# Values of the first two mLSTM heads in a buffer of their own, projected between the last HGRN steps

## The chip, the cores and the metric

One core of a Trainium2 chip runs the kernel. The metric is the device time of one execution in microseconds (us). Engines are named as in the profile: PE (matrix), DVE (vector), ACT (scalar), POOL (GpSimd), and SP, whose queue issues nearly all the DMAs.

## The reference

One layer of a diffusion backbone over 256 context and 1024 latent tokens of width 1024. Inputs are normalised and modulated by vectors that come from the conditioning, go through two bidirectional recurrent mixers of four heads each (HGRN2 and mLSTM), are mixed by an output matrix, and then go through PEER, a retrieval of single-neuron experts.

```python
def _modulate(x, shift, scale):
    return _layer_norm(x) * (1 + scale) + shift
...
o_hg_c, o_hg_l = _bidirectional(_gla_chunkwise, ...)
qk_l = jax.nn.silu(_conv_grid(jnp.concatenate([mq_l, mk_l], axis=-1), conv_w, conv_b))
h_ml_c, h_ml_l = _bidirectional(
    _mlstm_chunkwise, ml_shared(qk_c, mv_c), ml_shared(qk_l, mv_l),
    _mlstm_gates(mgt_c, gate_b), _mlstm_gates(mgt_l, gate_b))
...
x <- LN(alpha*x + gate1 * W_out [HGRN2 heads | mLSTM heads](modulate(LN(x))))
x <- LN(alpha*x + gate2 * PEER(modulate(LN(x))))
```

The mLSTM gates take a log-sigmoid of half of 16 gate columns; query and key of the mLSTM go through a 3x3 convolution over a 64-wide grid ahead of the recurrence; the values (mv) do not.

## The kernel before

The stages follow each other in program text, but the framework decides each engine's order with a timeline of its own, so work of one stage may lie in another's as far as buffers allow.

- `modcols` loads the first 2048 columns of w_mod (8 tiles of 1 MB) and multiplies them with the two conditioning vectors: 3 of 4 column blocks on PE, the fourth on DVE. Its result is `modc`, without which no token tile can be modulated. Two of the ten token tiles `xt` are loaded ahead of the weights, eight behind.
- `inputs_ln` normalises the tiles, transposes them on PE, modulates them on ACT into `xf`, and DVE and POOL write the pair `xmT` (fp16 high part, bf16 rest). Every projection runs three passes over high and low parts (`proj_f` with 512-column matmuls, line 222; `proj_t` with 256, line 230).
- A class `W` loads one 1 MB block of weights into `wf` and splits it: ACT casts the high part (line 76), POOL subtracts the rest (line 77). The blocks are named after their columns: HI, HQ, HF0, HF1, HG for HGRN, MQ, MK, MV, MO for the mLSTM.
- `gates` makes the mLSTM's gate rows on [64, 1280] tiles: transposes, log-sigmoid by three activations, scans on DVE; then 30 small transposes and 8 small matmuls (lines 331, 337) bring them back into columns.
- `modrows` multiplies the other 4096 columns of w_mod, 32 tiles of 512 KB in a buffer `wm` of its own, with 128 matmuls (line 686).
- `hgrn` projects values and runs 8 head-directions, each: gate projection, ACT functions (first `sg`, line 394), scan, and a recurrence on PE and DVE.
- `mlstm` projects values into one tile `mv` (`values(0)` for heads 0 and 1, `values(1)` for 2 and 3: 240 matmuls and 10 copies on ACT each). `qkproj` then copies query and key into `pad` (line 545) and convolves them with nine passes on DVE (lines 553 and 555). `one` runs the recurrence; POOL scales keys into `kw` (line 589) and adds the backward part to `acm` (line 647) from a single buffer `tm`. `ro.hg` and `ro.ml` are the readout's gates.
- `mix_weights` loads w_out by fourths into `wof` (three buffers), scales and splits it; `mix_out` and `peer` follow.
- `uprep` prepares 128 slices of PEER's table in spare time: load 512 KB into `us` (two buffers), ACT cast (line 198), POOL subtract (line 199), store `Ud`. 96 of them are called by `hgrn` and `mlstm` in program text; where they run is the framework's choice, in the same order on ACT, POOL and SP.

Of the kernel before, what the change touches and what calls it, by code (L numbers as in the profile page):

```python
# [236 lines left out]
def gates(g, I, w):  # L237
    nc, tc = g.nc, g.tc
    gp = g.gp
    with tc.tile_pool(name="gt", bufs=1, reuse_waits="tile") as tp:  # L240
        gb = tp.tile([128, 16], F32, name="gb")
        nc.sync.dma_start(gb, rowb(I["ml_gate_b"], 0, 16))
        ps = g.pp.tile([128, 512], F32, name="oa")
        for t in range(NT):
            proj_t(g, w, t, ps[:, t * 16:(t + 1) * 16])
        gt = tp.tile([128, NT, 2, 64], F32, name="gt")
        nc.vector.memset(gt, 0.0)
        psv = ps[:, :NT * 16].rearrange("p (t a d h) -> p t a d h", a=2, d=2, h=4)
        gbv = gb.rearrange("p (a d h) -> p a d h", a=2, d=2)
        for a in range(2):  # L250
            for d in range(2):
                nc.vector.tensor_tensor(gt[:, :, a, 32 * d:32 * d + 4], psv[:, :, a, d, :],
                                        gbv[:, None, a, d, :].to_broadcast([128, NT, 4]), op=OP.add)
        rows = []
        for a in range(2):
            r = tp.tile([64, SQ], F32, name=f"row{a}")
            for t0 in range(0, NT, 4):
                n = min(4, NT - t0)
                pt = g.pp.tile([128, 512], F32, name="sc")
                for i in range(n):  # L260
                    nc.tensor.transpose(pt[0:64, i * 128:(i + 1) * 128], gt[:, t0 + i, a, :], g.ident)
                nc.vector.tensor_copy(r[:, t0 * 128:(t0 + n) * 128], pt[0:64, :n * 128])
            rows.append(r)
        ir, fr = rows
        e = tp.tile([64, SQ], F32, name="ge")
        nc.scalar.activation(e, fr, AF.Abs)
        nc.scalar.activation(e, e, AF.Exp, scale=-1.0)
        nc.scalar.activation(e, e, AF.Ln, bias=1.0)
        lf = fr
        nc.vector.scalar_tensor_tensor(lf, fr, 0.0, e, op0=OP.min, op1=OP.subtract)  # L270
        one = tp.tile([64, NT, 128], F32, name="one")
        neg = tp.tile([64, NT, 128], F32, name="neg")
        nc.vector.memset(one, 1.0)
        nc.vector.memset(neg, 0.0)
        nc.vector.memset(one[:, :, 0:1], 0.0)
        nc.vector.memset(neg[:, :, 0:1], -BIG)
        oneF, negF = (x.rearrange("p t s -> p (t s)") for x in (one, neg))
        a = tp.tile([64, NT, 128], F32, name="ga")
        aF = a.rearrange("p t s -> p (t s)")
        nc.vector.tensor_tensor_scan(aF[0:32], oneF[0:32], lf[0:32], 0.0, op0=OP.mult, op1=OP.add)  # L280
        nc.vector.tensor_tensor_scan(aF[32:64, ::-1], oneF[32:64], lf[32:64, ::-1], 0.0, op0=OP.mult, op1=OP.add)
        gqF = ir
        gq = ir.rearrange("p (t s) -> p t s", s=128)
        nc.vector.tensor_sub(gqF, ir, aF)
        M = tp.tile([64, NT, 128], F32, name="gM")
        MF = M.rearrange("p t s -> p (t s)")
        nc.vector.tensor_tensor_scan(MF[0:32], negF[0:32], gqF[0:32], 0.0, op0=OP.add, op1=OP.max)
        nc.vector.tensor_tensor_scan(MF[32:64, ::-1], negF[32:64], gqF[32:64, ::-1], 0.0, op0=OP.add, op1=OP.max)
        G = tp.tile([64, NT], F32, name="gG")
        al = tp.tile([64, NT], F32, name="gal")  # L290
        nc.vector.tensor_copy(G[0:32], M[0:32, :, 127])
        nc.vector.tensor_copy(G[32:64], M[32:64, :, 0])
        nc.vector.tensor_copy(al[0:32], a[0:32, :, 127])
        nc.vector.tensor_copy(al[32:64], a[32:64, :, 0])
        mn = tp.tile([64, NT], F32, name="gmn")
        mp_ = tp.tile([64, NT], F32, name="gmp")
        nc.vector.tensor_tensor_scan(mn[0:32], G[0:32], al[0:32], 0.0, op0=OP.max, op1=OP.add)
        nc.vector.tensor_tensor_scan(mn[32:64, 1::-1], G[32:64, 1::-1], al[32:64, 1::-1], 0.0, op0=OP.max, op1=OP.add)
        nc.vector.tensor_tensor_scan(mn[32:64, :1:-1], G[32:64, :1:-1], al[32:64, :1:-1], mn[32:64, 0:1],
                                     op0=OP.max, op1=OP.add)  # L300
        nc.vector.memset(mp_, 0.0)
        nc.vector.tensor_copy(mp_[0:32, 1:NT], mn[0:32, 0:NT - 1])
        nc.vector.tensor_copy(mp_[32:64, 0:1], mn[32:64, 1:2])
        nc.vector.tensor_copy(mp_[32:64, NT - 1:NT], mn[32:64, 0:1])
        nc.vector.tensor_copy(mp_[32:64, 2:NT - 1], mn[32:64, 3:NT])
        ml = tp.tile([64, NT], F32, name="gml")
        nc.vector.tensor_max(ml, G, mp_)
        mpb = mp_[:, :, None].to_broadcast([64, NT, 128])
        nc.vector.tensor_tensor(M, M, mpb, op=OP.max)
        negM = tp.tile([64, LAT], F32, name="negM")  # L310
        nc.vector.tensor_scalar(negM, MF[:, CTX:], -1.0, None, op0=OP.mult)
        nc.sync.dma_start(g.negM, negM)
        win = tp.tile([64, LAT], F32, name="win")
        wv = fr.rearrange("p (t s) -> p t s", s=128)
        nc.vector.tensor_tensor(wv, mpb, M, op=OP.subtract)
        nc.scalar.activation(win, wv.rearrange("p t s -> p (t s)")[:, CTX:], AF.Exp)
        nc.sync.dma_start(g.win, win)
        ws = e.rearrange("p (t s) -> p t s", s=128)
        nc.vector.tensor_tensor(ws, gq, ml[:, :, None].to_broadcast([64, NT, 128]), op=OP.subtract)
        nc.scalar.activation(ws, ws, AF.Exp)  # L320
        cd = tp.tile([64, NT], F32, name="gcd")
        nc.vector.tensor_sub(cd, mp_, ml)
        nc.scalar.activation(cd, cd, AF.Exp)
        fl = a
        nc.vector.tensor_add(fl, a, M)
        nc.scalar.activation(fl, fl, AF.Exp, scale=-1.0)
# [1060 lines left out]
```

## Time and profile before

| what | us |
|---|---|
| median of 3 runs | 3220.53 (3216.59 to 3222.46) |
| profiled execution, its time | 3223.63 |
| profiled execution, its span | 3221.9 |
| mean granted clock of PE | 0.953 of full speed |
| PE busy in the span | 2938.5 |
| DVE busy in the span | 2611.8 |

The span runs from the first to the last instruction. About the first 886 us belong to the stages that the change touches; the part behind them is PEER and its preparation. Busy times are those of one execution.

### The profile page before, as it was taken

Reading aid. Unit: us, or ns where it says so; the run is one execution under the profiler, and the core shown is the slowest. Engines: PE = TensorE matmul, PEld = TensorE weight load, DVE = VectorE, ACT = ScalarE, POOL = GpSimd, SP = SyncE. Lnnn points to the kernel's source line nnn. Section 1 sums busy time; section 2 is a strip of 40 time slices with the busy share of each in tenths; the row PEclk is TensorE's granted clock in tenths of the full one; section 3 lists DMA queues with packets and bytes.
Section 4 is the critical chain, followed back from the end, with each engine's and each line's share of the span. In section 5 each row is a group of like instructions: output and inputs, shape, how many; then the busy total and the mean of one; then the engine's idle time right before and its main releaser. Section 6 shows DMA issues by size and latency. Waiting matters only on the chain.

```text
span 3221.9 us, 50811 instructions
## 1 busy us (share of the span) xinstructions
PE 2938.5 (91%) x18943; PEld 1892.4 (59%) x18943; DVE 2611.8 (81%) x5352; ACT 1181.8 (37%) x1699; POOL 1846.0 (57%) x1358
## 2 busy tenths in 40 slices
PE   7898989888898799799999989999999999999985
PEld 4644556657786567577777875555555555554432
DVE  8434464999878899888877777898999998988998
ACT  4465563324345532126666653222222222222111
POOL 3555675422347465416566665676666666666664
PEclk8899998898899899899999999999999999999987
DMA  7688666421267689758889998999999999999994
GB/s 282 213 289 291 213 207 232 139 64 55 103 221 268 210 324 331 288 176 279 300 278 297 307 345 324 355 368 364 359 364 360 360 354 366 355 347 336 342 327 183
DMA packets 319548, 900.33 MB, mean 279 GB/s; under 512 B 28076, under 2 KB 107572, under 8 KB 311364
## 3 DMA queue, kind: packets, MB, share of 16 engines
q1 hardware_dynamic: 208708, 494.38, 43.3%
q0 software_dynamic: 110592, 402.70, 34.2%
q8 instruction: 149, 2.44, 0.3%
q14 instruction: 99, 0.81, 0.1%
HBM read 758.67 MB, written 138.30 MB: 278 GB/s over the span
## 4 chain that ended last, share of the span: by engine, by line
PE 42%; DVE 24%; DMA 11%; POOL 9%; issue 9%; ACT 4%; SPq 0%; DVEq 0%; POOLq 0%; ACTq 0%
PE y L1164 16%; PE S L1131 12%; DMA row<-in_peer_v_dram,idx 5%; POOL row L1072 4%; DVE row L1091 3%; PE pj L222 3%; DVE mz L555 3%; PE pj L230 2%; DVE us L1034 2%; POOL vs L1147 2%; DMA us<-in_peer_ut_dram 2%; DMA row<-in_peer_u_dram,idx 2%; DVE hg L1099 2%; POOL uT L199 2%; PE y L1039 1%
## 5 line engine op out<-in xcount | busy, mean ns | idle before, releaser
L1164 PE MATMUL y<-vs,w 128*128 128x512 bf16 x3840 | 878.9, 382 | 40.5 <-POOL vs L1147 16.6
L1131 PE MATMUL S<-hTd,uT 128*128 128x320 f16 (+1 forms) x6144 | 898.6, 300 | 10.7 <-issue 6.2
L1131 PEld LDWEIGHTS <-uT 128*128 128x128 bf16 x6144 | 602.6, 98 | 276.0 <-issue 13.2
L1164 PEld LDWEIGHTS <-w 128*128 128x128 bf16 x3840 | 378.2, 98 | 471.4 <-issue 61.4
L1099 DVE SCALAR_TENSOR_TENSOR hg<-row,dot,hg 128x1024 f32<-128x1024 f32 x381 | 489.5, 1285 | 110.3 <-DMA row<-in_peer_v_dram,idx 94.7
L1072 POOL DMA_INDIRECT row<-in_peer_u_dram,idx x384 | 387.4, 1009 | 287.2 <-DVE row L1091 135.2
L1072 POOL DMA_INDIRECT row<-in_peer_v_dram,idx x384 | 387.4, 1009 | 219.7 <-DVE hg L1099 133.2
L1091 DVE SCALAR_TENSOR_TENSOR row<-row,hg 128x1024 f32<-128x1024 f32 x384 | 458.7, 1211 | 58.1 <-DMA row<-in_peer_u_dram,idx 52.1
L199 POOL TENSOR_TENSOR uT<-us,uT 128x1024 bf16<-128x1024 f32 x128 | 303.9, 2379 | 188.7 <-ACT uT L198 173.1
L1146 ACT CAST vs<-row 128x1024 bf16<-128x1024 f32 x128 | 133.5, 1043 | 488.7 <-DMA row<-in_peer_v_dram 467.0
L1147 POOL TENSOR_TENSOR vs<-row,vs 128x1024 bf16<-128x1024 f32 x128 | 277.9, 2171 | 28.7 <-ACT vs L1146 23.1
L1035 POOL TENSOR_TENSOR kT<-us,gf 128x512 f32<-128x512 bf16 x160 | 178.3, 1137 | 200.3 <-DVE us L1034 175.5
L222 PE MATMUL pj<-xmT,wb 128*128 128x512 f16 (+3 forms) x1248 | 262.5, 367 | 19.9 <-ACT pad L545 18.5
L1136 ACT ACTIVATE ge<-S 128x320 f32<-128x320 f32 x256 | 111.8, 441 | 408.2 <-PE S L1131 299.5
L230 PE MATMUL pj<-wb,xmT 128*128 128x256 f16 (+1 forms) x1728 | 224.3, 290 | 22.4 <-DVE rsg L748 12.0
L1171 DVE TENSOR_TENSOR ya<-ya,y 128x512 f32<-128x512 f32 x310 | 207.3, 681 | 26.1 <-PE y L1164 24.3
L230 PEld LDWEIGHTS <-xmT 128*128 128x128 f16 (+1 forms) x1968 | 186.6, 103 | 65.0 <-issue 24.1
L222 PEld LDWEIGHTS <-wb 128*128 128x128 f16 (+1 forms) x1248 | 123.8, 101 | 147.7 <-issue 43.3
L1040 ACT COPY gst<-y 128x512 f32<-128x512 f32 x160 | 171.3, 1075 | 83.9 <-PE y L1039 66.0
L1034 DVE TENSOR_TENSOR us<-iob,eT 128x512 bf16<-128x512 bf16 x320 | 172.4, 588 | 14.6 <-ACT kT L1036 9.0
L1039 PE MATMUL y<-kT 128*128 128x128 f32 x1280 | 165.2, 281 | 17.1 <-ACT kT L1036 8.1
L198 ACT CAST uT<-us 128x1024 bf16<-128x1024 f32 x128 | 133.2, 1044 | 122.9 <-DMA us<-in_peer_ut_dram 96.5
(390 smaller groups left out, 3927.8 us busy)
## 6 DMA issues: line engine op xcount, KB each, us to landing
us<-in_peer_ut_dram SPq DMA_DIRECT2D x128, 512.0 KB
Ud<-uT SPq DMA_DIRECT2D x128, 512.0 KB
uT<-Ud SPq DMA_DIRECT2D x128, 512.0 KB
row<-in_peer_v_dram SPq DMA_DIRECT2D x128, 512.0 KB
Gd<-gst SPq DMA_DIRECT2D x20, 1984.0 KB
Gt<-Gd SPq DMA_DIRECT2D x31, 1280.0 KB
Sd<-ge SPq DMA_DIRECT2D x66, 320.0 KB
kT<-Sd SPq DMA_DIRECT2D x66, 320.0 KB
```

The costliest lines, as they stand in the source:

```text
L199: nc.gpsimd.tensor_tensor(lo, uf, hi, op=OP.subtract)
L222: g.nc.tensor.matmul(ps[:, :t1 - t0], w.t[a][:, k, c0:c0 + 128], g.xmT[b][:, k, t0:t1], start=(k == 0 and a == b), stop=(k == KD - 1 and a ...
L230: g.nc.tensor.matmul(ps, g.xmT[a][:, k, t * 128:(t + 1) * 128], w.t[b][:, k, :w.n], start=(k == 0 and a == b), stop=(k == KD - 1 and a == 1))
L1034: nc.vector.tensor_tensor(cm[:, a], g.iob, eT[:, a, None, t0:t0 + 4].to_broadcast([128, 128, 4]), op=OP.is_equal)
L1039: nc.tensor.matmul(ps[:, i * 128:(i + 1) * 128], oh[:, 0, i], oh[:, 1, i], start=True, stop=True)
L1072: d = g.nc.gpsimd.indirect_dma_start(out=b, out_offset=None, in_=self.I["peer_u" if n < 128 else "peer_v"][0], in_offset=bass.IndirectOffs ...
L1091: nc.vector.scalar_tensor_tensor(b, b, 1.0, self.ps, op0=OP.mult, op1=OP.mult, accum_out=dot[:, j:j + 1])
L1099: nc.vector.scalar_tensor_tensor(self.ps, b, dot[:, j:j + 1], self.ps, op0=OP.mult, op1=OP.add)
L1131: m = nc.tensor.matmul(ps[:, :hn], uT[:, a, k, :], g.hTd[b][:, k, i * hn:(i + 1) * hn], start=(k == 0 and (a, b) == (0, 0)), stop=(k == KD ...
L1147: nc.gpsimd.tensor_tensor(v[:, 1], vf, v[:, 0], op=OP.subtract)
L1164: nc.tensor.matmul(ps, w[:, a, t * 128:(t + 1) * 128], v[:, b, h * 512:(h + 1) * 512], start=(n == 0), stop=(n == 3 * GI - 1))
L1171: nc.vector.tensor_add(ya, ya, ps)
```

## The change

- `modcols`: all ten token tiles are loaded ahead of w_mod; all four column blocks go to PE, into one PSUM bank at four partition offsets; four full transposes take the place of the small ones; the weights HI are loaded behind w_mod.
- `inputs_ln`: for odd blocks ACT writes the high part of `xmT` itself, with a second activation, where DVE copied it.
- `gates`: the log-sigmoid runs on [128, 80] before the transposes; transposes alternate between two banks; the small transposes into columns become a function `cols()`, called after both value projections of HGRN.
- `modrows` takes its tiles from the two `us` buffers that `uprep` uses too.
- `values(g, I, 0)` is called at the end of `hgrn` and writes `mv0`, which lies in a pool that outlives both stages; the other half is `mv1`.
- `mix_weights`: the first fourth uses `mv0`'s memory, the others share two buffers.

```diff
+    ps = g.pp.tile([128, 512], F32, name="pj", bufs=2)
+    xs = inputs_load(g, I, lp, 0, NT)
     for k in range(KD):
-        if k == KD // 2:
-            g.w0.append(W(g, I, HI))
         wt = mp.tile([128, 2048], F32, name="w0", bufs=8)
         nc.sync.dma_start(wt, I["w_mod"][0, k * 128:(k + 1) * 128, 0:2048])
-        for b in range(3):
-            nc.tensor.matmul(ps[b][0:2], g.cs[:, k::8], wt[:, b * 512:(b + 1) * 512], start=(k == 0), stop=(k == KD - 1))
...
+        for q in range(4):
+            nc.tensor.matmul(ps[32 * q:32 * q + 2], g.cs[:, k::8], wt[:, q * 512:(q + 1) * 512], start=(k == 0), stop=(k == KD - 1))
+    g.w0.append(W(g, I, HI))
+    for q in range(4):
+        o = slice(32 * q, 32 * q + 2)
+        (nc.scalar.copy if q % 2 else nc.vector.tensor_copy)(mr[o], ps[o])
...
-            nc.vector.tensor_copy(g.xmT[0][:, k, sl], f)
+            if k % 2:
+                nc.scalar.activation(g.xmT[0][:, k, sl], pt[:, :n * 128], AF.Identity, scale=g.modc[:, 8 + k, j:j + 1], bias=g.modc[:, k, j:j + 1])
+            else:
+                nc.vector.tensor_copy(g.xmT[0][:, k, sl], f)
...
+    nc.scalar.activation(e, f, AF.Abs)
+    nc.scalar.activation(e, e, AF.Exp, scale=-1.0)
+    nc.scalar.activation(e, e, AF.Ln, bias=1.0)
...
         inputs(1)
         g.uprep(8)
+        cols()
+        gs.close()
...
+        values(g, I, 0)
+
+
+def values(g, I, b):
+
+    nc = g.nc
+    nc.vector.memset(g.mv[b][:, :, :, 128:129], 1.0)
+    w = W(g, I, MV + 256 * b)
+    for t in range(NT):
+        ps = g.pp.tile([128, 512], F32, name="pj", bufs=2)
+        proj_t(g, w, t, ps[:, :256])
+        nc.scalar.copy(g.mv[b][:, t, :, 0:128], ps[:, :256].rearrange("p (h c) -> p h c", c=128))
...
-                wt = mp.tile([128, 1024], F32, name="wm", bufs=2)
+                wt = g.up.tile([128, 2, D], BF, name="us").rearrange("p a b -> p (a b)").bitcast(F32)
...
+        if h == 0:
+            wf = g.gp.tile([128, NT, 2, 129], F32, name="mv0").rearrange("p a b c -> p (a b c)")[:, 0:KD * 256]
+            wf = wf.rearrange("p (k c) -> p k c", c=256)
+        else:
+            wf = tp.tile([128, KD, 256], F32, name="wof", bufs=2)
...
+                g.mv = [g.gp.tile([128, NT, 2, 129], F32, name="mv0")]
```

The order of instructions moves at three places. On SP before, at the head of HGRN, the 32 tiles of w_mod (`wm`) are mixed with the loads (`us`) and stores (`Ud`) of `uprep`:

```order
L195 DMA us<-in_peer_ut_dram 128x1024
L202 DMA Ud<-uT 128x2048
L195 DMA us<-in_peer_ut_dram 128x1024
L677 DMA bb<-in_b_mod_dram 1x512 x4
L683 DMA wm<-in_w_mod_dram 128x1024 x2
L202 DMA Ud<-uT 128x2048
L195 DMA us<-in_peer_ut_dram 128x1024
L202 DMA Ud<-uT 128x2048
L195 DMA us<-in_peer_ut_dram 128x1024
L683 DMA wm<-in_w_mod_dram 128x1024 x2
L202 DMA Ud<-uT 128x2048
```

On SP in the changed kernel the w_mod tiles, now in `us`, come first, and the first load of `uprep` (`us<-in_peer_ut_dram`) stands behind the last of them:

```order
L207 DMA wf<-in_w_in_dram 128x2048
L691 DMA us<-in_w_mod_dram 128x1024 x4
L701 DMA mrow<-bb 1x512 x4
L685 DMA bb<-in_b_mod_dram 1x512 x4
L691 DMA us<-in_w_mod_dram 128x1024 x6
L207 DMA wf<-in_w_in_dram 128x2048
L691 DMA us<-in_w_mod_dram 128x1024 x8
L207 DMA wf<-in_w_in_dram 128x2048
L189 DMA us<-in_peer_ut_dram 128x1024 x2
L701 DMA mrow<-bb 1x512 x4
L196 DMA Ud<-uT 128x2048
```

All of w_mod has moved ahead of all of `uprep`: before, 23 slices were cast ahead of the split of HF1's first block, now none.

On ACT before, at the end of HGRN, the copies of the first mLSTM values (`mv`) stand behind the last head's last functions (`dec`, `qe`):

```order
L432 COPY km<-tr 128x512 x2
L432 COPY km<-tr 128x256
L198 CAST uT<-us 128x1024 x2
L420 ACTIVATE dec<-sg 128x20
L414 ACTIVATE qe<-sg 128x1024
L198 CAST uT<-us 128x1024 x4
L520 COPY mv<-pj 128x2x128 x2
L198 CAST uT<-us 128x1024 x2
L520 COPY mv<-pj 128x2x128
```

On ACT in the changed kernel the first copies (`mv_529` is `mv0`) stand between the last head's functions:

```order
L417 ACT_TABLE_LOAD
L417 ACTIVATE kt<-qt 128x1024
L426 ACTIVATE dec<-sg 128x20
L418 ACTIVATE qt<-qt 128x1024
L523 COPY mv_529<-pj 128x2x128
L424 ACTIVATE kh<-kh 128x1280
L495 COPY acc<-oa 128x4x128
L420 ACTIVATE qe<-sg 128x1024
L192 CAST uT<-us 128x1024
L523 COPY mv_529<-pj 128x2x128
L438 COPY km<-tr 128x512 x2
L192 CAST uT<-us 128x1024
```

The 240 matmuls of the values stand on PE accordingly between the last heads' steps, where before 48 of them stood there and 192 behind.

On POOL before, in the mLSTM, six slices of `uprep` stand between the splits of MV's second block (the first `wb` here) and MQ's second (the next), and none behind:

```order
L199 TENSOR_TENSOR uT<-us,uT 128x1024 x4
L77 TENSOR_TENSOR wb_5293<-wf,wb_5292 128x2048
L199 TENSOR_TENSOR uT<-us,uT 128x1024 x6
L77 TENSOR_TENSOR wb_5873<-wf,wb_5872 128x2048
L589 TENSOR_TENSOR kw<-mkm,gcol 128x1280 x2
L647 TENSOR_TENSOR acm<-acm,tm 128x2x128 x2
L77 TENSOR_TENSOR wb_6005<-wf,wb_6004 128x2048
L589 TENSOR_TENSOR kw<-mkm,gcol 128x1280
L647 TENSOR_TENSOR acm<-acm,tm 128x2x128 x2
L589 TENSOR_TENSOR kw<-mkm,gcol 128x1280
L77 TENSOR_TENSOR wb_6468<-wf,wb_6467 128x2048
L647 TENSOR_TENSOR acm<-acm,tm 128x2x128 x2
```

On POOL in the changed kernel, from ahead of the split of MQ's second block on (its row is the first `wb`, MK's second is the next):

```order
L193 TENSOR_TENSOR uT<-us,uT 128x1024 x7
L77 TENSOR_TENSOR wb_5852<-wf,wb_5851 128x2048
L193 TENSOR_TENSOR uT<-us,uT 128x1024 x2
L597 TENSOR_TENSOR kw<-mkm,gcol 128x1280
L193 TENSOR_TENSOR uT<-us,uT 128x1024 x4
L597 TENSOR_TENSOR kw<-mkm,gcol 128x1280
L193 TENSOR_TENSOR uT<-us,uT 128x1024 x2
L77 TENSOR_TENSOR wb_5984<-wf,wb_5983 128x2048
L193 TENSOR_TENSOR uT<-us,uT 128x1024
L655 TENSOR_TENSOR acm<-acm,tm 128x2x128
L193 TENSOR_TENSOR uT<-us,uT 128x1024
L597 TENSOR_TENSOR kw<-mkm,gcol 128x1280
```

Slices of `uprep` now lie between the `kw` and `acm` of the mLSTM's heads: in all 39 stand behind the split of MK's first block and ahead of that of MO's (before, 10).

## Rows read from the trace of the kernel before

**Rows 1.** Busy times by stretch, all engines; columns as its own heading says.

```profile
core 0: us, PE busy (x) PEld busy (x) DVE busy (x) ACT busy (x) POOL busy (x), PEclk, DMA share, GB/s
0.00:38.00 38.00, 27.52 (x87) 7.87 (x87) 26.52 (x58) 6.40 (x9) 4.50 (x6) 0.99 0.93 377
38.00:83.00 45.00, 33.30 (x346) 25.82 (x347) 44.79 (x79) 26.17 (x43) 28.07 (x16) 0.71 0.58 200
83.00:181.00 98.00, 85.30 (x649) 60.58 (x646) 38.03 (x46) 41.58 (x57) 53.00 (x22) 0.90 0.66 230
181.00:457.00 276.00, 250.98 (x1416) 133.53 (x1414) 135.90 (x166) 164.28 (x193) 177.16 (x75) 0.95 0.73 253
457.00:518.00 61.00, 54.06 (x312) 38.91 (x308) 34.72 (x61) 23.14 (x27) 39.29 (x18) 0.75 0.54 185
...
553.00:620.00 67.00, 52.32 (x282) 30.94 (x281) 64.62 (x43) 24.44 (x31) 33.69 (x11) 0.88 0.58 202
620.00:740.00 120.00, 103.91 (x698) 75.20 (x697) 107.98 (x247) 37.67 (x52) 28.46 (x13) 0.93 0.18 49
740.00:886.00 146.00, 121.19 (x977) 105.22 (x976) 127.80 (x381) 58.83 (x78) 42.95 (x21) 0.91 0.25 86
```

**Rows 2.** Timeline: first DVE modc, then the first gate activation on ACT.

```profile
37.97 0.11 DVE L135 TENSOR_SCALAR modc<-modc 128x16 f32<-128x16 f32 x1
...
181.34 0.38 ACT L394 ACTIVATE sg<-pj 128x256 f32<-128x256 f32 x1 [0.70 <-PE pj L222]
```

**Rows 3.** Groups by line and shape, 38 to 83 us.

```profile
L180 ACT ACTIVATE xf<-tr,modc 128x512 f32<-128x512 f32 x8 | 6.1, 777 | 5.6 <-DVE xmT L182 4.6 <-POOL xmT L182 1.1
...
L180 ACT ACTIVATE xf<-tr,modc 128x256 f32<-128x256 f32 x4 | 2.1, 557 | 1.4 <-DVE lnrs L150 0.7 <-DVE xmT L182 0.7
```

**Rows 4.** Timeline of PE at the two gate transposes; idle before in brackets.

```profile
125.61 0.34 PE L331 MATMUL sc<-ident,row 64*128 64x64 f32 x1 [5.12 <-DVE row L284]
...
142.03 0.36 PE L331 MATMUL sc<-ident,ge 64*128 64x64 f32 x1 [6.40 <-ACT ge L320]
```

**Rows 5.** Busy time of line 686 alone (w_mod matmuls), by stretch.

```profile
181.00:335.00 154.00, 30.43 (x116) 2.59 (x116) 0.97 0.80 280
```

**Rows 6.** Groups by line, 181 to 457 us: the w_mod matmuls.

```profile
L686 PE MATMUL tr<-wm,cs 128*1 128x512 f32 x116 | 30.4, 621 | 8.4 <-DMA wm<-in_w_mod_dram 8.4
```

**Rows 7.** Busy time of line 230 alone (value projections), by stretch.

```profile
457.00:518.00 61.00, 5.32 (x41) 3.77 (x41) 0.75 0.54 185
518.00:544.00 26.00, 23.26 (x192) 19.36 (x192) 0.93 0.76 258
```

**Rows 8.** Waits, 544 to 620 us.

```profile
DVE mz L553 <- ACT pad L545: 22.9, 1, 22.9
```

**Rows 9.** Busy time of line 199 alone (uprep's subtract) by stretch.

```profile
181.00:457.00 276.00, 115.13 (x47) 0.95 0.73 253
...
546.00:620.00 74.00, 26.82 (x10) 0.89 0.60 207
620.00:886.00 266.00, 0.00 (x0) 0.92 0.22 69
```

**Rows 10.** Chain of waits from 545 to 620 us.

```profile
by line: DVE mz L555 64.4%; PE pj L222 12.4%; DVE mz L553 6.2%; PE pj L230 2.8%; DVE mz L565 2.8%; PE sc L583 2.3%; issue 2.2%; PE tr L576 2.1%; DVE qw L623 1.7%; ACT mz L557 1.5%; DVE mz L567 1.1%; ACT pad L545 0.8%
...
555.67 1.30 DVE mz L555
...
559.63 3.05 DVE mz L555
```

**Rows 11.** Timeline of POOL, 552 to 572 us.

```profile
552.95 2.13 POOL L199 TENSOR_TENSOR uT<-us,uT 128x1024 bf16<-128x1024 f32 x1 [1.00 <-ACT uT L198]
558.64 2.94 POOL L199 TENSOR_TENSOR uT<-us,uT 128x1024 bf16<-128x1024 f32 x1 [3.56 <-ACT uT L198]
```

**Rows 12.** Groups of DVE by line and shape, 546 to 620 us.

```profile
L555 DVE SCALAR_TENSOR_TENSOR mz<-pad,cwT,mz 128x1024 f32<-128x1024 f32 x30 | 56.1, 1886 | 0.5
```

**Rows 13.** Chain of waits from 835 to 890 us.

```profile
841.15 6.40 DMA wof<-in_w_out_dram
```

More of the change, by code (lines that the diff above doesn't have):

```diff
@@ L135, in modcols @@
+    for b in range(4):
+        nc.tensor.transpose(pt[:, b * 128:(b + 1) * 128], mr[:, b * 128:(b + 1) * 128], g.ident)
+    nc.vector.tensor_tensor(g.modc.rearrange("p (q b) j -> p b q j", q=4),
+                            pt.rearrange("p (b q r) -> p b q r", b=4, r=32)[:, :, :, 0:2],
+                            bT.rearrange("p (q b) -> p b q", q=4)[:, :, :, None].to_broadcast([128, 4, 4, 2]), op=OP.add)
     nc.vector.tensor_scalar(g.modc[:, 8:16, :], g.modc[:, 8:16, :], 1.0, None, op0=OP.add)
@@ L234, with gates @@
 SEG = ((0, CTX), (CTX, CTX + 512), (CTX + 512, SQ))
-def gates(g, I, w):
+def gates(g, I, w, tp):
     nc, tc = g.nc, g.tc
     gp = g.gp
[L240 to L326, printed above, removed]
@@ new lines, in gates @@
+    nc.vector.tensor_tensor(f, psv[:, :, 1], gbv[:, None, 1].to_broadcast([128, NT, 2, 4]), op=OP.add)
+    nc.scalar.activation(e, f, AF.Abs)
+    nc.scalar.activation(e, e, AF.Exp, scale=-1.0)
+    nc.scalar.activation(e, e, AF.Ln, bias=1.0)
+    for d in range(2):
+        nc.vector.tensor_tensor(gt[:, :, 0, 32 * d:32 * d + 4], psv[:, :, 0, d, :],
+                                gbv[:, None, 0, d, :].to_broadcast([128, NT, 4]), op=OP.add)
+        nc.vector.scalar_tensor_tensor(gt[:, :, 1, 32 * d:32 * d + 4], f[:, :, d], 0.0, e[:, :, d], op0=OP.min, op1=OP.subtract)
@@ new lines, in gates @@
+    rows = []
+    for a in range(2):
+        r = tp.tile([64, SQ], F32, name=f"row{a}")
+        for t0 in range(0, NT, 4):
+            n = min(4, NT - t0)
+            pt = g.pp.tile([128, 512], F32, name=("sc", "up")[t0 // 4 % 2])
+            for i in range(n):
+                nc.tensor.transpose(pt[0:64, i * 128:(i + 1) * 128], gt[:, t0 + i, a, :], g.ident)
+            nc.vector.tensor_copy(r[:, t0 * 128:(t0 + n) * 128], pt[0:64, :n * 128])
+        rows.append(r)
+    ir, fr = rows
+    e = tp.tile([64, SQ], F32, name="ge")
@@ new lines, in gates @@
+    lf = fr
+    one = tp.tile([64, NT, 128], F32, name="one")
+    neg = tp.tile([64, NT, 128], F32, name="neg")
+    nc.vector.memset(one, 1.0)
+    nc.vector.memset(neg, 0.0)
+    nc.vector.memset(one[:, :, 0:1], 0.0)
+    nc.vector.memset(neg[:, :, 0:1], -BIG)
+    oneF, negF = (x.rearrange("p t s -> p (t s)") for x in (one, neg))
+    a = tp.tile([64, NT, 128], F32, name="ga")
+    aF = a.rearrange("p t s -> p (t s)")
+    nc.vector.tensor_tensor_scan(aF[0:32], oneF[0:32], lf[0:32], 0.0, op0=OP.mult, op1=OP.add)
@@ new lines, in gates @@
+    mpb = mp_[:, :, None].to_broadcast([64, NT, 128])
+    nc.vector.tensor_tensor(M, M, mpb, op=OP.max)
+    negM = tp.tile([64, LAT], F32, name="negM")
+    nc.vector.tensor_scalar(negM, MF[:, CTX:], -1.0, None, op0=OP.mult)
+    nc.sync.dma_start(g.negM, negM)
+    win = tp.tile([64, LAT], F32, name="win")
+    wv = fr.rearrange("p (t s) -> p t s", s=128)
+    nc.vector.tensor_tensor(wv, mpb, M, op=OP.subtract)
+    nc.scalar.activation(win, wv.rearrange("p t s -> p (t s)")[:, CTX:], AF.Exp)
@@ L327, in gates, with cols @@
+    nc.sync.dma_start(g.win, win)
+    ws = e.rearrange("p (t s) -> p t s", s=128)
+    nc.vector.tensor_tensor(ws, gq, ml[:, :, None].to_broadcast([64, NT, 128]), op=OP.subtract)
+    nc.scalar.activation(ws, ws, AF.Exp)
+    cd = tp.tile([64, NT], F32, name="gcd")
+    nc.vector.tensor_sub(cd, mp_, ml)
+    nc.scalar.activation(cd, cd, AF.Exp)
+    fl = a
+    nc.vector.tensor_add(fl, a, M)
+    nc.scalar.activation(fl, fl, AF.Exp, scale=-1.0)
+    def cols():
         g.col = gp.tile([128, NT, 3, 2, 4], F32, name="gcol")
@@ L339, in gates @@
         nc.vector.tensor_copy(g.cd, pb[:, :8 * NT].rearrange("p (r t) -> p r t", t=NT))
+    return cols
 def hgrn(g, I, w0, w1):
@@ L369, in hgrn @@
         v = vp.tile([128, NT, 512], F32, name="hv")
-        gates(g, I, w1)
-        modrows(g, I, es.enter_context(tc.tile_pool(name="mr", bufs=1, reuse_waits="tile")))
+        mr = es.enter_context(tc.tile_pool(name="mr", bufs=1, reuse_waits="tile"))
+        gs = es.enter_context(ExitStack())
+        cols = gates(g, I, w1, gs.enter_context(tc.tile_pool(name="gt", bufs=1, reuse_waits="tile")))
+        modrows(g, I, mr)
         def inputs(b):
```

81 lines of the change are left out of this document (47 added, 34 removed).

## The prediction

> **What bounds the kernel now.** I read the busy times by stretch first, then the groups of lines and the chain of waits inside the stretches that the change touches. [rows 1] cut the first 886 us into stages, and each has another limit. To 38 us the DMA engines are 93% busy: the loads of w_mod and the tiles set when `modc` is ready, at 38 us [rows 2]. From 38 to 83 DVE is busy 44.79 of 45 us: the layer norm waits for DVE. From 83 to 457 it is PE: 85.30 of 98 us, then 250.98 of 276. From 457 to 518, HGRN's tail, PE shows 54.06 of 61 us, but at a granted clock of 0.75: that stretch waits more than the busy share tells. From 553 on it is DVE, 64.62 of 67 us, 107.98 of 120 and 127.80 of 146. So what the change takes from PE counts up to 518 us, and what it adds to DVE counts behind 553 us. The profiled execution took 3223.63 us, 3.1 us more than the median of the three runs (3220.53). I sum against it and take 3.1 off at the end.
>
> **The start and the layer norm.** By [rows 1] the DMAs moved 377 GB/s over 38 us, 14.3 MB. Now all ten tiles (5.2 MB) and all eight blocks (8.4 MB) stand ahead of `modc`, 13.6 MB; at the 0.41 MB/us of a queue without its idle first 3 us, which I estimate from that row (14.3 MB in 35 us), the last block lands at 36 us. Behind it stand four matmuls, the copies to SBUF, of which the second on ACT is queued behind the cast of HI's block (1.05 MB at that rate, 2.6 us, and the cast, for which I put 2: an estimate), and the transposes: `modc` at about 43 us, 5 later. In exchange the statistics and the scaling of all tiles are done by then, and a fourth of the copies to `xmT` that DVE made (half of 24) go to ACT. The limit becomes ACT's 36 activations (12 for each of three token groups, 4 of the 12 new). By [rows 3] they cost 777 ns for 512 columns and 557 ns for 256: 24 x 0.78 + 12 x 0.56 = 25.4 us. The stage ends at 43 + 25 = 68 us instead of 82 to 83: -14 us. Bounds: 0, if DVE or PSUM banks still pace it; -17, if activations overlap as their starts in that stretch allow.
>
> **The gate waits.** PE stood 5.12 and 6.40 us at the transposes of line 331 [rows 4], because they stand in PE's order ahead of the projections while DVE still made the rows. `cols()` is now behind both projections. That is -11.5 us of PE idle in a stretch where PE is the limit; I take -10. Bounds 0 and -11.5.
>
> **The w_mod matmuls.** Their work stays: 116 in 30.43 us [rows 5], of which PE waited 8.4 us for `wm` [rows 6]. In the changed order 60 of 128 stand ahead of the first `sg`, at 181 us [rows 2] in the old trace, where 12 stood; the others follow behind it, so the sum of PE's work to the end of HGRN is unchanged, and only the wait can go. The tiles no longer share the queue with `uprep`, but still have two buffers. I take -5, half the wait and a little; bounds 0 and -8.4. Together these three make -29 us, with bounds 0 and -37.
>
> **values(0).** Of its 240 matmuls 41 lay in the tail and 192 took 23.26 us behind it [rows 7], and DVE idled 22.9 us for the first `pad` [rows 8]: those 23 us were on the path. Now they fill the last heads. The tail can hold some of them free: 7 us of PE idle [rows 1], and a clock that rises from 0.75 towards 0.95 would shorten its 54 us by 11. That is 18 us of room, and the ends are 0 and -23. I take -15.
>
> **wof.** The readout's chain ends in 6.40 us of loading `wof` [rows 13]. One of the four loads now starts when `mv0` is free, ahead of this. Its wait goes only in part, since DVE is behind by then too: -3, bounds 0 and -6.4.
>
> **uprep in the mLSTM.** This is what the change costs. `uprep` starts behind all of w_mod on SP, so HGRN takes 35 slices where 60 were cast ahead of MV's first block, and 39 instead of 10 come behind MK's split: 29 more, in stretches where DVE is the limit. Before, none ran from 620 to 886 us, and 10 from 546 to 620 [rows 9]. In the conv a pass of line 555 takes 1.30 us alone and 3.05 us [rows 10] beside the subtract that begins at 558.64 and is drawn out to 2.94 [rows 11]: 1.75 us lost. Over the stretch line 555 has 30 passes of 1886 ns [rows 12]: 30 x (1.886 - 1.30) = 17.6 us lost while POOL was busy for 33.69 [rows 1], or 0.52 for each us of it; a subtract, 2.13 us alone [rows 11], took 26.82 / 10 = 2.68 there [rows 9]. So one takes 0.52 x 2.68 = 1.4 us from DVE, and at most the 1.75 of the single pass: I take 1.5, and 29 make 43 us. DVE is idle 12 of 120 and 18 of 146 us [rows 1], which can swallow a ninth, 5 us; queueing of `kw` and `acm` behind two or three subtracts adds some 2. Net +40. Bounds: +15, if most fall where DVE waits anyway; +54, if none does and they cost 1.75 each plus the queue.
>
> By the Trainium skill, "SBUF — State Buffer", section "Who interferes with whom", DVE and GpSimd share one port pair as an exclusive lock: a DVE instruction with two SBUF inputs blocks fully against a GpSimd instruction that reads SBUF. The row of 3.05 us agrees in kind, and its loss of 1.75 us is a little under one subtract. By the rule alone each of the 29 could cost its whole length. The sum would then lie on the slow side, which is the second rival below.
>
> **Sum.** -29 - 15 - 3 + 40 = -7 us: 3223.6 becomes 3216.6 in an execution like the profiled one, and 3213 as the median, 0.2% less.
>
> **Rivals.** *The casts cost less (faster).* Slices may fall into DVE's idle time, PSUM-sourced passes of the recurrence may not be hit, and HGRN, with 25 fewer, frees POOL. [rows 9] speak for it in that HGRN's 47 subtracts cost 115.13 us of POOL, 2.45 each; [rows 12] against it, since the conv is hit. With +15 instead of +40 the sum is -32: 3188.
> *The casts cost all their length (slower).* DVE in the mLSTM stands still for each added subtract: 29 x 2.13 = 62 us instead of 40, so -47 + 62 = +15: 3235. It decides from 47 / 29 = 1.62 us per subtract on, and the 1.75 us of a single pass [rows 10] is above that. Against it: the mean over the conv is lower, and DVE has idle time behind 620 us.
> *The values don't fit (the change doesn't do what it says).* The matmuls between the last heads' steps lengthen the tail by as much as they took behind it, since PE is already 89% busy there [rows 1]: 0 instead of -15, sum +8, 3228.
> *Gain and loss cancel* within 0.2%, which is part of the forecast's own spread.
>
> **How the numbers follow.** 0.2% (6.4 us) is about what a measurement of this kernel can tell from no change. Forecast 0.45, its own range 3202 to 3226: 0.27 of it faster, 0.15 within the bound, 0.03 slower. Cheap casts 0.20, all faster. Dear casts 0.20: 0.18 slower, 0.02 within. Values that don't fit 0.15: 0.07 slower, 0.07 within, 0.01 (with cheaper casts) faster. Sum: faster 0.48, same 0.24, slower 0.28. The range reaches to the cheap casts on one side and to the dear ones on the other, 3187 to 3236, and leaves out the outer halves of both.
>
> **What would show it.** In the changed profile: `modc` at 42 to 44 us, the layer norm over before 70, no wait of PE on the gates' rows, the first `sg` at 165 to 177 us, the first `pad` copied some 45 us earlier, no idle DVE ahead of it, `mv0` copies inside HGRN, and then an mLSTM that takes some 40 us longer from the first `pad` to `mix_out`, with passes of line 555's counterpart near 3 us beside subtracts. The prediction is wrong if the mLSTM grows by under 20 or over 55 us, if PE waits for w_mod's tiles ahead of the first `sg`, or if the tail of HGRN grows by the values' 23 us.

## The result, and the profile after

The changed kernel takes 3256.98 us (median of 4 runs, 3250.82 to 3260.78) where the kernel before took 3221.49 (4 runs): a ratio of 1.0103 on record, 95% interval 1.0081 to 1.0125 (the two medians alone give 1.0110). It is slower by 1.0%, outside the range of the prediction. The profiled execution took 3250.82 us, the fastest of the four, 27 us more than that of before.

The busy times by stretch, with boundaries at the same events as in [rows 1] (the end of the layer norm, the first and the last `sg`, the first `pad`, the first `kw`; 38, 740 and 866 us are no events), read:

```profile
core 0: us, PE busy (x) PEld busy (x) DVE busy (x) ACT busy (x) POOL busy (x), PEclk, DMA share, GB/s
38.00:73.00 35.00, 27.22 (x310) 21.93 (x303) 20.35 (x38) 26.62 (x43) 12.22 (x10) 0.79 0.22 72
73.00:190.00 117.00, 112.30 (x809) 62.16 (x808) 39.69 (x53) 23.16 (x44) 18.00 (x6) 1.00 0.52 163
190.00:447.00 257.00, 229.35 (x1323) 134.88 (x1322) 133.41 (x166) 165.43 (x195) 171.71 (x75) 0.93 0.62 213
447.00:522.00 75.00, 71.42 (x529) 50.00 (x530) 32.26 (x58) 31.61 (x42) 46.41 (x22) 1.00 0.62 217
522.00:604.00 82.00, 58.46 (x316) 34.98 (x315) 76.64 (x59) 29.86 (x39) 44.88 (x16) 0.85 0.62 212
604.00:740.00 136.00, 95.79 (x581) 64.78 (x579) 128.21 (x234) 51.46 (x63) 76.29 (x33) 0.87 0.63 214
740.00:866.00 126.00, 105.02 (x847) 92.07 (x848) 106.58 (x317) 57.38 (x74) 37.21 (x20) 0.91 0.23 77
```

The events themselves in the timeline, on DVE, ACT and PE: the end of `modc`, the first `sg`, the first `pad`, and the first matmul of `mix_out` (the first two of before are in [rows 2]):

```profile
45.00 2.08 DVE L126 TENSOR_SCALAR modc<-modc 128x16 f32<-128x16 f32 x1
...
190.74 0.38 ACT L400 ACTIVATE sg<-pj 128x256 f32<-128x256 f32 x1
...
522.63 1.21 ACT L553 COPY pad<-pj 128x512 f32<-128x512 f32 x2 [0.86 <-DVE pad L542]
...
908.75 1.01 PE L845 MATMUL pj<-wo,mT 128*128 128x256 f16 x5 [0.95 <-ACT mT L82]
```

and the last two in the kernel before:

```profile
552.78 0.58 ACT L545 COPY pad<-pj 128x512 f32<-128x512 f32 x1
...
886.58 0.60 PE L833 MATMUL pj<-wo,mT 128*128 128x256 f16 x4
```

`modc` is ready at 47 us, 9 later than before. The layer norm ends at 73 (10 earlier), the first `sg` is at 190.7 (9 later), the last `sg` begins at 446.9 (10 earlier than 456.9), the first `pad` at 522.6 (30 earlier than 552.8). Then the lead turns: the first `kw` is 18 us early, the last one 18 late, and `mix_out` begins at 908.8, where it was at 886.6. From the first `pad` to `mix_out` it now takes 386.1 us, 52.3 more than the 333.8 before. What comes behind took 2340 us, 5 more.

The groups of PE from 73 to 190 us show what the first `sg` waits for: PE is busy 112.3 of 117 us at full granted clock, and 120 of the 128 records of w_mod stand in it, 31.8 us, with 1.2 us of waiting for their tiles.

```profile
L224 PE MATMUL pj<-wb,xmT 128*128 128x256 f16 (+1 forms) x420 | 50.3, 274 | 3.4 <-ACT hv L382 3.4
L694 PE MATMUL tr<-us,cs 128*1 128x512 f32 x120 | 31.8, 591 | 1.2 <-DMA us<-in_w_mod_dram 1.2
L216 PE MATMUL pj<-xmT,wb 128*128 128x512 f16 (+3 forms) x124 | 26.1, 359 | 0.0
```

In the mLSTM, from 522 to 758 us, the groups of DVE and POOL by line, and the subtract of `uprep` by stretch (before, [rows 9] and [rows 12]):

```profile
L563 DVE SCALAR_TENSOR_TENSOR mz<-pad,cwT,mz 128x1024 f32<-128x1024 f32 x60 | 111.8, 1880 | 0.3
L626 DVE SCALAR_TENSOR_TENSOR dm<-bM,gcol,mlm 128x128 f32<-128x128 f32 x40 | 25.8, 700 | 5.5 <-DMA bM<-negM 4.2 <-PE ob L639 1.2
...
L193 POOL TENSOR_TENSOR uT<-us,uT 128x1024 bf16<-128x1024 f32 x37 | 90.9, 2457 | 89.6 <-ACT uT L192 88.3 <-DMA bM<-negM 1.2
...
core 0: us, POOL busy (x), PEclk, DMA share, GB/s
522.00:604.00 82.00, 34.71 (x13) 0.85 0.62 212
604.00:758.00 154.00, 55.99 (x24) 0.87 0.62 211
```

37 subtracts lie in these stretches (36 of their casts behind the first `pad`), and 60 passes of the convolution take 1.88 us each; in the kernel before it was 1.88 only in the first 30 of them [rows 12], and 1.68 over all from the first `pad` to 743 us. The small operations grow as well: line 626 takes 700 ns (409 before, as line 618). The two groups in the kernel before:

```profile
L555 DVE SCALAR_TENSOR_TENSOR mz<-pad,cwT,mz 128x1024 f32<-128x1024 f32 x61 | 102.0, 1683 | 0.6
L618 DVE SCALAR_TENSOR_TENSOR dm<-bM,gcol,mlm 128x128 f32<-128x128 f32 x32 | 11.6, 409 | 1.3 <-PE ob L631 1.2
```

DVE is busy 76.64 of 82 and 128.21 of 136 us there, nearly without a gap. One place on both engines, 536 to 552 us, shows single passes beside POOL's subtracts (`uT` of line 193, `wb` of line 77):

```profile
536.47 10.67 DVE L563 SCALAR_TENSOR_TENSOR mz<-pad,cwT,mz 128x1024 f32<-128x1024 f32 x4
547.06 2.61 DVE L561 TENSOR_SCALAR mz<-pad,cwT 128x1024 f32<-128x1024 f32 x1
549.59 3.14 DVE L563 SCALAR_TENSOR_TENSOR mz<-pad,cwT,mz 128x1024 f32<-128x1024 f32 x1
...
538.22 2.82 POOL L193 TENSOR_TENSOR uT<-us,uT 128x1024 bf16<-128x1024 f32 x1 [3.80 <-ACT uT L192]
541.01 5.05 POOL L77 TENSOR_TENSOR wb<-wf,wb 128x2048 bf16<-128x2048 f32 x1
546.01 5.63 POOL L193 TENSOR_TENSOR uT<-us,uT 128x1024 bf16<-128x1024 f32 x2
```

### The profile page after: what moved, and what is told of

Read it like the earlier page. It is cut to its first block, busy times and chain, and to the rows that moved or that the text cites. A ratio compares the mean times of both kernels' runs of the same rounds, so it can differ in the third digit from the quotient of the medians.

```text
span 3249.0 us, 50773 instructions
## 1 busy us (share of the span) xinstructions
PE 2923.4 (90%) x18935; PEld 1875.6 (58%) x18935; DVE 2610.9 (80%) x5325; ACT 1188.8 (37%) x1717; POOL 1845.5 (57%) x1359
## 4 chain that ended last, share of the span: by engine, by line
PE 34%; DVE 28%; DMA 13%; issue 9%; POOL 8%; ACT 5%; another core or an unknown queue 1%; SPq 0%; DVEq 0%; POOLq 0%; ACTq 0%
PE y L1176 12%; PE S L1143 10%; DMA row<-in_peer_v_dram,idx 6%; POOL row L1084 4%; DVE hg L1111 3%; DVE mz L563 3%; DVE row L1103 3%; PE pj L216 3%; PE pj L224 2%; POOL vs L1159 2%; DVE us L1046 2%; DMA us<-in_peer_ut_dram 2%; PE y L1051 1%; POOL uT L193 1%
```

## The experiments

All times are medians and ratios to the kernel before on the same chip; chips differ (3210 to 3225 us for the kernel before). The events in us are read from the timeline of each run's trace, one execution each. "Slices" are the casts of `uprep` between the first `pad` and `mix_out`.

| run | ratio, 95% interval | first sg | last sg | first pad | mix_out | slices | pad to mix_out |
|---|---|---|---|---|---|---|---|
| before | 1 | 181.3 | 456.9 | 552.8 | 886.6 | 8 | 333.8 |
| changed | 1.0103 (1.0081 to 1.0125) | 190.7 | 446.9 | 522.6 | 908.8 | 36 | 386.1 |
| e1_wm_gt | 1.0102 (1.0076 to 1.0127) | 262.6 | 515.0 | 590.2 | 917.5 | 0 | 327.3 |
| e2_before_us | 1.0035 (1.0015 to 1.0055) | 185.8 | 445.8 | 540.5 | 898.7 | 31 | 358.2 |
| e3_act_low | 0.9960 (0.9941 to 0.9979) | 190.9 | 446.9 | 528.5 | 857.5 | 35, none on POOL | 328.9 |
| e4_start_only | 0.9988 (0.9967 to 1.0008) | 181.0 | 458.8 | 545.8 | 879.2 | 7 | 333.4 |
| w8_before | 0.9875 (0.9859 to 0.9891) | 183.1 | 433.6 | 520.1 | 854.9 | 8 | 334.8 |
| values_late | 1.0019 (1.0007 to 1.0032) | 191.1 | 453.4 | 545.9 | 908.4 | 32 | 362.5 |
| wm_half | 0.9986 (0.9974 to 0.9999) | 195.9 | 477.7 | 558.4 | 897.4 | 11 | 339.0 |
| modrows_late | 1.0186 (1.0162 to 1.0209) | 188.2 | 439.1 | 516.5 | 951.2 | 13 | 434.7 |
| w8_after | 0.9939 (0.9915 to 0.9962) | 177.6 | 433.9 | 508.5 | 865.7 | 20 | 357.2 |
| start_us | 1.0081 (1.0061 to 1.0102) | 188.8 | 451.4 | 546.1 | 911.1 | 34 | 365.0 |
| before_mr_ml | 0.9962 (0.9949 to 0.9974) | 180.4 | 432.3 | 520.1 | 877.7 | 8 | 357.6 |
| after_mr_ml | 0.9963 (0.9950 to 0.9976) | 189.4 | 438.7 | 516.1 | 888.9 | 13 | 372.8 |

**Do POOL's subtracts cost the mLSTM its time?**

```diff
-            nc.gpsimd.tensor_tensor(lo, uf, hi, op=OP.subtract)
+            if 57 <= i2 < 96:
+                nc.scalar.copy(lo, uf)
+            else:
+                nc.gpsimd.tensor_tensor(lo, uf, hi, op=OP.subtract)
```

> The changed kernel, in which the low part of slices 57 to 95 is not the difference but a copy made by ACT, so that these 39 slices keep their place, their loads, casts and stores but leave POOL. Theory A1, that they cost by DVE and POOL taking turns: passes of the convolution return to 1.3 us, the stretch from the first pad to mix_out falls from 386 to 340 to 350 us, 3210 to 3222. Rival A2, that they cost by queues on ACT or SP or by their transfers: the stretch stays above 375 us, 3245 or more.

The stretch fell from 386.1 to 328.9 us, 57 less, and the time to 3214.04 us against 3224.62. The slices were there, with their loads, casts and stores, and cost next to nothing: the stretch is as long as in e1_wm_gt (327.3 us), which has no slice in it. The group of the convolution on DVE in it, 528 to 711 us:

```profile
L566 DVE SCALAR_TENSOR_TENSOR mz<-pad,cwT,mz 128x1024 f32<-128x1024 f32 x61 | 77.4, 1283 | 0.4
```

A pass of the convolution takes 1.28 us (1.88 in the changed kernel). DVE's busy time from `pad` to `mix_out`, summed over the stretches, is 283.3 us here, 346.5 in the changed kernel: 63 us for 36 subtracts, 1.75 each, which is the length that the single passes of [rows 10] lost. Theory A1 holds, and the stretch fell further than its 340 to 350 us.

**Is the delay of the slices by w_mod's tiles the cause?** Two ways: the tiles out of `us` in the changed kernel (`wq` is the gates' pool), and into `us` in the kernel before.

```diff
-                wt = g.up.tile([128, 2, D], BF, name="us").rearrange("p a b -> p (a b)").bitcast(F32)
+                wt = wq.tile([128, 1024], F32, name="wm", bufs=2)
```

> The changed kernel with w_mod's tiles in a buffer wm of their own (two, in the gates' pool) and no longer in uprep's us; all 96 slices then stand ahead of the first kw, as in the kernel before. Theory A, that w_mod in us delays uprep and the 27 delayed slices cost the mLSTM 47 us beside its DVE work: the first pad stays near 525 to 540 us, the stretch from the first pad to mix_out falls from 386 us to about 335, and the time is 3195 to 3212 us. Rival B, that the mLSTM is longer for another part of the change (values early, mv0, wof): that stretch stays above 370 us and the time above 3240. Rival C, that HGRN pays for the slices what the mLSTM saves: the first pad at 550 or later, 3215 to 3235.

The stretch fell by 59 us to 327.3, as theory A has it, but the time did not fall: the first `sg` came 72 us later, and the first `pad` at 590, where theory A had 525 to 540. That lies in the range of rival C, but PE did not wait for slices. The gates' pool gives its memory to the heads, so they waited for all of w_mod, and PE for its tiles: 36.6 us, the first row of its waits from 73 to 262 us.

```profile
PE tr L695 <- DMA wm<-in_w_mod_dram: 36.6, 10, 5.2
```

The run tells the mLSTM's part and not the whole.

```diff
-                wt = mp.tile([128, 1024], F32, name="wm", bufs=2)
+                wt = g.up.tile([128, 2, D], BF, name="us").rearrange("p a b -> p (a b)").bitcast(F32)
```

> The kernel before with one edit: w_mod's tiles in us. Theory A: the backlog appears by this edit alone (35 slices ahead of MV's first block, as in the changed kernel), w_mod's matmuls move ahead of the first sg, and the stretch from the first pad to mix_out grows from 334 to 375 to 390 us; 3255 to 3275. Rival B: under 3230. Rival C, that HGRN gives back what the mLSTM loses: 3225 to 3245.

The edit alone brings the backlog (31 slices) and a longer mLSTM (+24), but less than expected; the first `pad` comes 12 us earlier, and 9 us are lost, not 34 to 54. The time lies in the range of rival C: HGRN gives back half of what the mLSTM loses. More is lost when all of the changed modcols and inputs_ln is added:

```diff
-    xs = inputs_load(g, I, lp, 0, 2)
+    xs = inputs_load(g, I, lp, 0, NT)
...
-                wt = mp.tile([128, 1024], F32, name="wm", bufs=2)
+                wt = g.up.tile([128, 2, D], BF, name="us").rearrange("p a b -> p (a b)").bitcast(F32)
```

> The kernel before with three parts of the change: modcols, inputs_ln, and w_mod in us; gates, cols, values and w_out's loads as before. If the parts add up: mix_out at 890 us (899 with w_mod in us alone, 7 less for the start), 1.001 to 1.004 of the kernel before. Rival, that the earlier start turns into more slices in the mLSTM: mix_out at 898 to 910.

The parts do not add up: `mix_out` is at 911 instead of 890, a ratio of 1.0081. The rival's time holds, its reason in part: the first slice is cast at 206 us (191 in e2_before_us), 34 stand behind the `pad`, and of the 12 us by which `mix_out` comes later than in e2_before_us some 7 lie in the mLSTM and the rest ahead of it. `mix_out` is as late here as in the whole changed kernel (908.8).

**Does the new start help at all?** modcols and inputs_ln alone, on the kernel before:

> The kernel before with the changed modcols and inputs_ln alone. If the earlier end of the layer norm (about 11 us) passes on through the stretch in which PE is the limit: first sg at 168 to 174 us and 3208 to 3216. Rival, that it is absorbed ahead of the first pad by slices, weights and waits that do not start earlier: 3218 to 3225.

The first `sg` did not move, and the ratio shows no gain clear of its interval; the 7 us by which `pad` and `mix_out` come earlier in the one trace arise behind the last `sg`. The end of the layer norm, the last write to `xmT` on DVE, lies at 82 us here, and at 71 in e2_before_us, which has the old start but no slices beside it:

```profile
78.75 3.22 DVE L176 TENSOR_TENSOR xmT<-xf,xmT 128x512 bf16<-128x512 f32 x2
```

and of e2_before_us:

```profile
70.70 0.69 DVE L182 TENSOR_TENSOR xmT<-xf,xmT 128x512 bf16<-128x512 f32 x1
```

So the 10 us by which the changed kernel's layer norm ends earlier come from the slices that are gone from it, not from the new start.

**Is HGRN bound by PE, and what do w_mod's matmuls cost where they stand?** Seven of eight blocks left out, in either kernel:

```diff
-        for k in range(KD):
+        for k in range(1):
...
-                                     start=(k == 0), stop=(k == KD - 1))
+                                     start=(k == 0), stop=True)
```

> The kernel before with one of modrows' eight blocks of w_mod only: 28 of 32 tiles and 112 of 128 matmul records are left out, so the second half of the modulation is not what the reference computes; the order of slices stays. If PE is the limit of HGRN, as the prediction's sum had it: the stretch from the first to the last sg falls by 27 us of matmuls and 7 us of waits, from 275 to about 241, and the time to 3185 to 3195. If w_mod's matmuls lay half in gaps that other waits leave open, as the changed kernel's 256 us from first to last sg suggests: 255 to 262 us, and 3203 to 3213.

The stretch from the first to the last `sg` fell by 25 us to 250.5, between the two cases; `mix_out` came 32 us earlier, and the ratio fits the time of the first case. Of w_mod's 30.4 us of matmuls and 8.4 us of waits in HGRN [rows 5, 6] most lay on the path, and about a third did not.

> The changed kernel with one of modrows' eight blocks only: 28 of 32 tiles and 112 of 128 matmul records are left out, so the second half of the modulation is not what the reference computes. In the order 22 slices instead of 39 then stand behind MK's split. Theory, that the first sg waits for PE alone and that w_mod's matmuls ahead of it cost their full length: first sg at 160 to 168 us instead of 191; that a delayed slice costs the mLSTM 1.6 to 1.8 us: 350 to 362 us from the first pad to mix_out instead of 386. Together mix_out some 55 us earlier and 0.98 to 0.99 of the kernel before. Rival: first sg at 180 us or later, as in the run that called modrows late, because copies on ACT that stand behind slices hold PE up.

The mLSTM behaves as expected (357.2 us with 20 slices), but the first `sg` came only 13 us earlier, between the theory's 28 and the rival's 11 or less: PE then waited 11.4 us for the gates' ACT chain, the first row of its waits from 73 to 178 us. In the changed kernel w_mod's matmuls cover that wait. So `mix_out` came 43 us earlier, not 55, and the ratio is outside the expected 0.98 to 0.99.

```profile
PE up L329 <- ACT ge L316: 11.4, 1, 11.4
```

**What do the early values bring?** Their call back in the mLSTM, `mv0` and `mv1` in its pool, w_out's loads as before:

```diff
-        values(g, I, 0)
...
-        g.mv.append(vp.tile([128, NT, 2, 129], F32, name="mv1"))
+        g.mv = [vp.tile([128, NT, 2, 129], F32, name=f"mv{b}") for b in range(2)]
+        values(g, I, 0)
```

> The changed kernel with the first two heads' values back in the mLSTM's own pool and place, and w_out's loads back in three buffers; the backlog of slices stays. If the change's shorter way from the last sg to the first pad (76 us after 96) is this part's: it returns to 93 to 97 us, and the time grows to 3270 to 3280. Rival: the later start of the mLSTM gives slices time to run ahead of it, and its stretch shrinks by as much: 3250 to 3262.

From the last `sg` to the first `pad` it took 92.5 us again (75.8 in the changed kernel), but `mix_out` is at 908.4 instead of 908.8: the mLSTM is shorter by the same 24 us. The 96th slice is cast at 749 us here and at 744 in the changed kernel. From the first to the 96th a slice comes every 5.7 and 5.8 us in these two and every 5.9 in the kernel before, whatever stage runs beside it: the slices keep their own pace, and an mLSTM that starts earlier spends more of its time beside them. The ratio of 1.0019 is lower than the equal `mix_out` lets expect, and below both cases; the rest lies behind it (below).

**Versions that might beat both.** w_mod in half tiles in a buffer of its own:

```diff
+            for q in range(4):
+                wt = mp.tile([128, 512], F32, name="wm", bufs=2)
...
-            for x in range(2):
-                wt = g.up.tile([128, 2, D], BF, name="us").rearrange("p a b -> p (a b)").bitcast(F32)
```

> The changed kernel with w_mod in a buffer of its own again, in half tiles of 256 KB (two of them), in a pool that holds nobody else up; the slices stand as in the kernel before (60 ahead of MV's first block, 96 ahead of the first kw). Theory A: first sg at 168 to 176 us, first pad at 515 to 530 us, 330 to 340 us from there to mix_out, 3190 to 3205. Rival, that without the backlog HGRN pays for the slices and w_mod together: first pad at 540 or later, 3210 to 3225.

No backlog and a short mLSTM, but the rival holds for the front: with slices beside the layer norm and w_mod in HGRN the first `pad` came at 558. The median of 3206.40 us, on a chip where the kernel before takes 3210.11, is 0.1% below it.

modrows called late:

```diff
-        modrows(g, I, mr)
...
+        modrows(g, I, vp)
         cw = vp.tile([80, 128], F32, name="cw")
```

> The changed kernel with modrows called at the head of the mLSTM, behind all slices, still in us. Theory A: no w_mod in the gates or HGRN and no backlog, so first sg at 160 to 170 us, first pad at 495 to 515 us; PE has 13 to 15 per cent of idle time in the mLSTM to take 31 us of matmuls, 335 to 350 us from pad to mix_out, 3180 to 3200. Rival, that PE's order puts matmuls that wait for their tiles ahead of the mLSTM's: over 365 us from pad to mix_out, 3210 or more.

The rival holds: PE waited 70.7 us for w_mod's tiles ahead of the mLSTM's first `kw`, the first row of its waits from 516 to 684 us, and the stretch grew to 434.7 us.

```profile
PE tr L693 <- DMA us<-in_w_mod_dram: 70.7, 24, 41.5
```

One head later, where the slices are done, in the kernel before and in the changed one, the tiles in `us` in both:

```diff
                 if (hh, e) == (0, 1):
+                    modrows(g, I, vp)
                     values(1)
```

> The kernel before with modrows called in the mLSTM, between its first and its second head, from us, where all slices are done and PE has 13 to 17 per cent idle. If the matmuls of w_mod fit into that: HGRN gains what leaving them out gained (mix_out at 855 to 868 us), 0.986 to 0.993 of the kernel before. Rival, that PE's order makes the mLSTM wait for the tiles: over 360 us from the first pad to mix_out, 1.000 or more.

> The changed kernel with modrows called in the mLSTM, between its first and its second head, from us. No backlog and no w_mod in the gates and HGRN: first pad at 500 to 520 us, 335 to 355 us from there to mix_out, 0.983 to 0.993 of the kernel before. Rival, as for the kernel before with this edit: over 370 us, 1.000 or more.

Both beat the kernel before, by 0.4% each (3207.13 and 3211.12 us against 3221.51; the intervals leave out 1), and so the changed one too. From the first to the last `sg` they take 24 and 26 us less than before, from the first `pad` to `mix_out` 24 and 39 us more: the matmuls fit into the mLSTM only in part. `mix_out` at 877.7 lies between the two cases expected for the first; the second has the long stretch of its rival (372.8 us) and yet a ratio near the theory's.

## Why the prediction was wrong

Busy times from the first `pad` to `mix_out`, on which the first point rests, in this order of the kernel before, the changed kernel, values_late and e3_act_low (the means are over four parts of the stretch):

```profile
sum 333.80, PE 278.23 PEld 211.99 DVE 300.87 ACT 121.14 POOL 105.16; mean PE 69.56 PEld 53.00 DVE 75.22 ACT 30.28 POOL 26.29
...
sum 386.10, PE 288.20 PEld 215.18 DVE 346.51 ACT 153.16 POOL 175.67; mean PE 72.05 PEld 53.80 DVE 86.63 ACT 38.29 POOL 43.92
...
sum 362.50, PE 284.74 PEld 213.38 DVE 333.64 ACT 144.44 POOL 163.86; mean PE 71.19 PEld 53.35 DVE 83.41 ACT 36.11 POOL 40.97
...
sum 329.00, PE 274.34 PEld 209.77 DVE 283.26 ACT 183.79 POOL 83.81; mean PE 68.58 PEld 52.44 DVE 70.81 ACT 45.95 POOL 20.95
```

- **The mLSTM, the largest term, was mis-sized: +52 us from the first `pad` to `mix_out`, not +40.** The mechanism was right: 28 more slices lie behind the first `pad` (29 in the order), POOL's subtract is what costs (e3_act_low), and the delay comes with w_mod in `us` (e1_wm_gt, e2_before_us). The price of one, "I take 1.5", was near: DVE's busy time grew by 45.6 us over the kernel before, 1.63 for each of the 28 (1.75 for each of all 36 against e3_act_low). The step that failed is that DVE's idle time "can swallow a ninth, 5 us": it grew, from 32.9 us before to 39.6. That makes some 10 of the 12 us that are missing. The subtracts did not bring this idle time, for without them it is 45.7 (e3_act_low). With the values late, 24 slices more than before lengthen the mLSTM by 28.7 us only: DVE pays 1.37 for each and has 28.9 us of idle time, so there the forecast's price and its discount come out nearly as they were put. At 52 us the changed kernel is past the 47 from which the rival of dear casts decides.
- **The three terms of the front gave -10 us at the last `sg`, not -29.** Here steps failed, not only sizes. First, "60 of 128 stand ahead of the first `sg`" mixed units: the program has 64 matmuls in line 686, not 128, and the trace has two records for each of these fp32 ones, so 60 of 64 stand there, 120 records and 31.8 us: 108 records more than the 12 before, not 48. With them the first `sg` came at 190.7 us, where 165 to 177 was forecast. Second, "the sum of PE's work to the end of HGRN is unchanged, and only the wait can go": the work was the same, but in HGRN part of it had filled waits that are open again. PE is idle 27.6 of 257 us there, where it was 25 of 276 with 8.4 us of `wm` in them; and in w8_before, where nearly all of this work is gone, HGRN is only 25 us shorter. Third, the layer norm ended 10 us earlier, not 14, and not by the new start (e4_start_only; 71 us in e2_before_us with the old one).
- **The gate waits went as forecast:** no wait of PE on the gates' rows is left from 73 to 190 us. But w_mod's matmuls took their place; without them 11.4 us of such a wait return (w8_after).
- **The values shortened the way to the first `pad` by 20 us, 15 forecast (17 against values_late), and it bought nothing:** with them late, `mix_out` comes at the same time, and the ratio is even lower. That a gain ahead of a paced backlog is spent inside it was in no term and in no rival: the sum adds -15 for the values and +40 for the slices as if they were independent.
- **wof:** from the last `kw` to `mix_out` it took 78 us (74 before), so no gain shows.

Put together at `mix_out`: -30 at the first `pad` and +52 behind it make +22, where -7 was forecast; the profiled execution adds 5 behind `mix_out`, and the median of four lies 6 above that execution.

By the Trainium skill, "SBUF — State Buffer", section "Who interferes with whom", the blocked engine stands still for the whole instruction of the other. The runs are below that: for each subtract, 2.13 us alone, DVE paid 1.75 us against e3_act_low, and 1.3 to 1.6 for each added slice against the kernel before.

**What stays open.** For equal events at `mix_out` the stretch behind it took 2340 us in the changed kernel and 2307 in values_late, on another chip (where the kernel before is 11 us faster). The framework orders PEER's instructions otherwise in the two. But ACT's order there is the same in values_late as in e2_before_us, start_us and before_mr_ml, which took 2330 to 2333 us on other chips, so the order alone does not explain it; how much belongs to the chip is not separated. Nor is it settled why 36 slices cost 24 us more in the changed kernel than 32 in values_late: some 13 of them are busy time of DVE, where four slices at 1.75 us make 7, and some 11 are idle time. The two kernels differ by the place of the values and the buffers of w_out, but wm_half, which has the early values too, has 31.9 us of idle time, no more than the kernel before; so the place of the values alone does not explain it.

## What to carry to other kernels

A buffer that two streams share puts one behind the other in the queue: ask where the delayed stream will then run, and what the engine that bounds that stretch pays for each of its instructions when they overlap. A single disturbed row gives the size of that price and not its bound: it lost 1.75 us, and over these runs an added slice lengthened the mLSTM by 1.1 to 2.0 us. When work leaves an early stage, ask whether a later stage waits for a backlog with a pace of its own; if so, an earlier start is no gain. Before counts from a program's order are multiplied by durations from a trace, compare the two counts for the same line.

## What the runs showed of the hardware

A subtract of `uprep` on POOL stretches DVE's casts and subtracts of the layer norm too: in e4_start_only a subtract of 128x512 on DVE takes 2.49 us beside one of 2.29 on POOL at 74 us, and 0.69 without (e2_before_us, above). With slices beside it the stage ended at 82 to 84 us in eight kernels, without them at 71 to 73 in six, with the old start and the new. The length of the mLSTM with slices beside it was, over the runs that have no w_mod in it, 0 to 11 slices: 327 to 339 us; 20: 357; 31 to 34: 358 to 365; 36: 386; 35 without POOL: 329. So the price of a slice is not one number.
